# The first two stages of a one-core decoder block, put in order by hand on four engines

## The chip, the cores and the metric

The kernel runs as one program on one core of a Trainium2 chip. The metric is the device time of one execution in microseconds (us), the median of several runs. Engines are named as in the profile: PE (TensorE; PEld is its weight load), DVE (VectorE), ACT (ScalarE), POOL (GpSimd) and SP (SyncE, which here only issues DMAs). DVEq, SPq and so on are the sequencers that issue DMAs.

## What is computed

One transformer block on 256 tokens of width 1024, all in float32. Cut to what matters here:

```
cond = silu(c)                                   # c: 1024
shift_m, scale_m, gate_m, shift_f, scale_f, gate_f = split(cond @ ada_w + ada_b)
h = rmsnorm(x, norm_mix_g) * (1 + scale_m) + shift_m          # 256 x 1024
p = h @ w_in            # q, compressed/selected/window keys and values, gates, MLA parts, merge gates
o_nsa = sparse attention with T5 bias over compressed, selected and window keys
o_mla = latent attention with rotary keys (cos/sin of positions)
x = x + gate_m * ((sigmoid(p.merge_a) * o_nsa + sigmoid(p.merge_b) * o_mla) @ w_o)
h = rmsnorm(x, norm_ffn_g) * (1 + scale_f) + shift_f
x = x + gate_f * (silu(conv3(h @ w_gate)) * (h @ w_up)) @ w_down
return rmsnorm(x, final_norm_g)
```

## The kernel before, in words

Activations lie transposed: 8 tiles of 128 channels by 256 tokens. Every product is made from three matmuls in a reduced float32 form: each operand is split into a high part (a rounding copy, on ACT) and a low part (operand minus high part, on DVE), and `mm3` adds high by high, high by low, low by high.

**Opening.** `par` (a table of biases, norms and c) and the identity (a slice of `cst`) are loaded on ACT's queue, x on SP's in four quarters. From c come `cond` (a tanh on ACT, two operations on DVE), then eight PE matmuls against the identity that spread `cond` over all partitions, then `crow`, their copy out of PSUM. x is squared (ACT), added up (DVE), reduced on PE; the reciprocal root is taken on ACT and POOL (`rstd_col`) and spread over the partitions by a PE matmul (`rstd_bc`, its result `rsp`). Some warm-up matmuls (`busy(WARM[i])`) stand between.

**Stage A, the first projection.** It runs over 8 blocks k of 128 input channels. `modulate(k)` loads two 512 KB pieces of `adaA`, reduces each with `crow` on DVE (`gemv`, an operation of 128x1024), makes the scale `am` and the shift `mod`, then `hf` (x by scale by rsp, DVE), its high part `hh` (ACT) and its low part `hl` (DVE). Then two weight chunks (c = 0, 1) of 128x1024 from `wA` are split into `hi` and `lo`, and each makes 8 tiles of output, 24 matmuls. All 16 output tiles are held in the 8 PSUM banks `accA` (lg, lg, pt, pt, o, mm, mm, ms) until k = 7.

**Evacuation and the values' stage.** The banks are then emptied: `k_evac` (pt banks, keys), `t_evac` (lg banks, inputs of the compressed branch, after which POOL adds position terms), `q_evac` (o, mm, ms banks, queries). The values' stage needs the lg and pt banks again: for 8 blocks k a chunk of 128x560 from `wvg` is split, and 12 matmuls of 280 columns go into four banks (`vps`). The bias table is loaded by four 512 KB DMAs of 1 KB rows from `vdr` (`BT`).

**Mixing stage.** Sparse attention of eight head pairs (`Pair`), with other work (compression with `cw1`, latent projections, merge gates, further `gemv`s) filled in between, then latent attention, the output projection and the gated MLP.

A list scheduler decides the order on every engine before, from priorities (`prio`), dependences and a few `issue_after`s; each engine then runs its list strictly in that order. A tile pool has a fixed number of buffers for a name (`RB = 5` for `raw`, `HB = 3` for `hi` and `lo`); who allocates the next one waits until the oldest is free.

## Time and profile before

| | |
|---|---|
| median of 3 runs | 460.11 us (457.87, 460.11, 460.21) |
| the profiled execution | 458.63 us, of which the span from the first to the last instruction is 456.8 us |
| granted TensorE clock, mean | 0.992 of full speed |
| PE busy | 439.2 us, 96% of the span |
| DVE busy | 366.5 us, 80% |
| ACT busy | 282.3 us, 62% |
| HBM read | 96.01 MB |

Busy time of PE is no measure of its speed, because the matmuls overlap: how many start in a stretch says more. A wait is read from the start times of rows that follow each other on one engine.

### The profile page before, as it was taken

The page shows a single profiled execution, that of the slowest core. Times are in us where ns is not written, and L with a number is a line of the kernel's source. Part 1 is how long each engine was busy: PE and PEld are TensorE (multiplying, and loading weights), DVE is VectorE, ACT ScalarE, POOL GpSimd, SP SyncE. Part 2 cuts the span into 40 slices and gives each one's busy share as a digit, 9 for nine tenths or more (in the row PEclk, how much of TensorE's full clock was granted, in tenths as well). Part 3 has the DMA queues.
Part 4 walks back from the last instruction along what each step waited for, and adds up shares of the span by engine and source line. Part 5 has one row for each costly group of instructions (what it writes and reads, how often), then busy time and mean ns, then how long its engine had stood idle before and what let it go on. Part 6 is the DMA issues. An engine that isn't in the chain of part 4 may idle for free.

```text
span 456.8 us, 9366 instructions
## 1 busy us (share of the span) xinstructions
PE 439.2 (96%) x3514; PEld 414.5 (91%) x3514; DVE 366.5 (80%) x873; ACT 282.3 (62%) x610; POOL 26.2 (6%) x45
## 2 busy tenths in 40 slices
PE   6999989999989999999999999999999999999994
PEld 6899978777869879999989999999999999999993
DVE  3899988878788878899989888778778778778643
ACT  4444475879698996656657776556556556546332
POOL 1100042030010111000000000000000000000001
PEclk9899999999999999999999999999999999999998
DMA  7999898779762337997857875655655655653002
GB/s 279 414 406 377 252 311 238 290 269 297 261 213 95 101 121 250 305 317 254 296 206 220 252 259 189 194 179 178 193 185 168 199 187 165 204 187 93 1 0 93
DMA packets 31565, 99.33 MB, mean 217 GB/s; under 512 B 4293, under 2 KB 6933, under 8 KB 31520
## 3 DMA queue, kind: packets, MB, share of 16 engines
q1 hardware_dynamic: 30208, 96.59, 62.7%
q0 software_dynamic: 1024, 1.98, 1.9%
q8 instruction: 28, 0.46, 0.4%
q10 hardware_dynamic: 288, 0.17, 0.2%
q14 instruction: 17, 0.14, 0.1%
HBM read 96.01 MB, written 1.14 MB: 213 GB/s over the span
## 4 chain that ended last, share of the span: by engine, by line
PE 79%; DVE 6%; DMA 6%; ACT 4%; issue 2%; POOL 1%; DVEq 0%; POOLq 0%; SPq 0%; ACTq 0%
PE mm L176 29%; PE lg L176 12%; PE o L176 12%; PE ms L176 11%; PE pt L176 10%; DMA ad<-in_adaR 3%; DMA cst<-in_cst 2%; PE pt L860 2%; DVE lo L136 2%; DVE ad L377 1%; ACT hi L135 1%; ACT pt L864 1%; PE ms L221 1%; ACT s L608 0%; DVE s L449 0%
## 5 line engine op out<-in xcount | busy, mean ns | idle before, releaser
L176 PE MATMUL mm<-s,hi 128*128 128x256 f32 x552 | 105.2, 288 | 0.6 <-DVE s L991 0.3
L136 DVE TENSOR_TENSOR s<-raw,s 128x1024 fp32r<-128x1024 f32 x66 | 80.5, 1221 | 17.9 <-PE mm L176 14.5
L176 PE MATMUL mm<-s,s 128*128 128x258 f32 (+1 forms) x544 | 94.1, 283 | 0.0
L176 PEld LDWEIGHTS mm<-s,hi 128*128 128x128 f32 x552 | 85.3, 189 | 3.7 <-issue 1.2
L135 ACT ACTIVATE s<-raw 128x1024 fp32r<-128x1024 f32 x66 | 69.0, 1051 | 23.2 <-PE mm L176 23.2
L176 PEld LDWEIGHTS mm<-s,s 128*128 128x128 f32 x544 | 77.6, 189 | 0.1
L176 PE MATMUL mm<-s,lo 128*128 128x256 f32 x268 | 76.9, 287 | 0.1
L136 DVE TENSOR_TENSOR lo<-raw,hi 128x1024 fp32r<-128x1024 f32 (+2 forms) x55 | 63.5, 1161 | 5.6 <-ACT hi L135 5.4
L135 ACT ACTIVATE hi<-raw 128x1024 fp32r<-128x1024 f32 (+2 forms) x55 | 53.5, 989 | 21.0 <-PE mm L176 6.8
L176 PEld LDWEIGHTS mm<-s,lo 128*128 128x128 f32 x268 | 50.5, 188 | 1.5 <-issue 0.7
L176 PE MATMUL o<-s,s 128*128 128x258 f32 (+1 forms) x272 | 47.8, 283 | 0.0
L377 DVE CUSTOM_DVE_ANT_0 ad<-ad,crow 128x1024 f32<-128x1024 f32 x36 | 43.6, 1218 | 3.2 <-DMA ad<-in_adaR 2.9
L176 PE MATMUL ms<-s,s 128*128 128x258 f32 x264 | 46.1, 283 | 0.0
L176 PEld LDWEIGHTS o<-s,s 128*128 128x128 f32 x272 | 39.0, 189 | 0.0
L176 PEld LDWEIGHTS ms<-s,s 128*128 128x128 f32 x264 | 37.7, 189 | 0.0
L176 PE MATMUL lg<-zh,s 128*128 128x256 f32 x176 | 34.7, 280 | 0.0
L176 PE MATMUL pt<-zh,s 128*128 128x256 f32 x176 | 34.6, 279 | 0.0
L839 ACT ACTIVATE L<-L,sm 128x128 f32<-128x128 f32 (+1 forms) x64 | 28.3, 449 | 1.4 <-DVE sm L835 1.4
L176 PEld LDWEIGHTS lg<-zh,s 128*128 128x128 f32 x176 | 28.6, 188 | 0.0
L176 PEld LDWEIGHTS pt<-zh,s 128*128 128x128 f32 x176 | 28.5, 188 | 0.0
L835 DVE CUSTOM_DVE_ANT_0 L<-lg,s 128x128 f32<-128x128 f32 (+1 forms) x64 | 20.9, 350 | 8.6 <-PE lg L176 8.0
L176 PE MATMUL lg<-s,s 128*128 128x256 f32 (+4 forms) x104 | 27.3, 350 | 0.5 <-DVE sm L835 0.5
(250 smaller groups left out, 810.4 us busy)
## 6 DMA issues: line engine op xcount, KB each, us to landing
ad<-in_adaR SPq DMA_DIRECT2D x32, 512.0 KB, 4.6
raw<-in_wg SPq DMA_DIRECT2D x22, 512.0 KB, 3.5
raw<-in_wu SPq DMA_DIRECT2D x22, 512.0 KB, 4.4
raw<-in_wd SPq DMA_DIRECT2D x22, 512.0 KB, 4.5
raw<-in_wA SPq DMA_DIRECT2D x16, 512.0 KB, 8.0
raw<-in_wm SPq DMA_DIRECT2D x16, 512.0 KB, 4.9
L<-in_adaA SPq DMA_DIRECT2D x12, 512.0 KB, 7.9
raw<-in_cw SPq DMA_DIRECT2D x8, 512.0 KB, 5.3
```

Of the source, the lines that this page charges most:

```text
L135: nc.scalar.activation(hi[:], raw[:], AF.Copy)
L136: nc.vector.tensor_tensor(lo[:], raw[:], hi[:], ALU.subtract)
L176: nc.tensor.matmul(o, l, r, start=start, stop=stop, **kw)
L221: m = nc.tensor.matmul(self.ps[:, tt:tt + 1], sq[:, tt * 128:tt * 128 + 128], ones[:, 0:1], start=first and tt == 0, stop=last, skip_group ...
L377: nc.vector.tensor_tensor_reduce(out=ad, in0=ad, in1=crow[:], scale=1.0, scalar=0.0, op0=ALU.mult, op1=ALU.add, accum_out=dst)
L835: nc.vector.tensor_tensor_reduce(out=L[:, br, j, 0:nk], in0=lgj[:, br, :], in1=bias_view(2 * t + j, qt), scale=1.0, scalar=3e38, op0=ALU.a ...
L839: nc.scalar.activation(L[:, br, j, 0:nk], L[:, br, j, 0:nk], AF.Exp, scale=-1.0, bias=sm[:, i:i + 1], accum_out=sm[:, 4 + i:5 + i])
L860: nc.tensor.transpose(pt[:, (kb * 2 + j) * 128:(kb * 2 + j) * 128 + 128], self.L[qt][:, br, j, kb * 128:kb * 128 + 128], ident)
L864: nc.scalar.activation(self.PT[qt, br][:, 0:qt + 1, :], pt[:, 0:(qt + 1) * 256].rearrange("p (b q) -> p b q", b=qt + 1), AF.Copy)
```

## The change

`opening()` and everything from `modulate(0)` to the end of the values' stage stand inside `tc.manual_schedule` for DVE, ACT, PE and SP: on these four engines the instructions run in the order in which the code is written; POOL and all later stages are still ordered by the list scheduler. Inside, the following differ:

- The identity becomes 128 more columns of `par`; one load, first on SP's queue. x comes in two loads.
- `crow` is copied by DVE instead of ACT; four additions of squares instead of five, each reduced on its own; `vec` is made by ACT instead of DVE; the scaled identity of `rstd_bc` by ACT instead of DVE; `am` and `mod` by ACT instead of DVE; `sb1` by POOL with the factor `norm_mix_g` folded in.
- The first six weight chunks are loaded early into other buffers; `HB` is 4.
- For k = 0 all high-by-high matmuls come first, then high-by-low, then low-by-high. The chunks c = 0 of k = 6 and 7 come before their chunks c = 1, so that lg and pt banks are complete 48 matmuls before the others.
- In the values' stage one `q_evac` half and one split stand in each block; the pt banks come first.
- The bias loads `BT` are issued after the third chunk of the values' weights; the tables, later `adaR` loads and `w2k` wait for that stage's end.

```diff
-N_A = 16
-WARM = (6, 3, 4)
+WARM = (5, 2, 2, 3, 3)
-HB = 3
+HB = 4
-EV = "k1 q1 t0 q3 q2 k0 d q0 t1"
-TE = "avvvaaav"
+TE = "aaaavvaa"
...
+        def fetch(early=False):
+            src, cols, _, _ = chunks.pop(0)
+            raw = s4(F32, (128, cols)) if early else st.tile([128, cols], F32, tag="raw", name=nm("raw"), bufs=RB)
+            raws.append([raw])
+            return nc.sync.dma_start(raw[:], src).ins
+        def head():
+            raw = raws[0][0]
+            raws[0] += [st.tile(raw.shape, F32R, tag=t, name=nm(t), bufs=HB) for t in ("hi", "lo")]
+            nc.scalar.activation(raws[0][1][:], raw[:], AF.Copy)
+        def rest():
+            raw, hi, lo = raws.pop(0)
+            nc.vector.tensor_tensor(lo[:], raw[:], hi[:], ALU.subtract)
+            return hi, lo
...
-        nc.scalar.dma_start(par[:], a["par"])
-        nc.scalar.dma_start(ident, a["cst"][:, C_ID:C_ID + 128])
-        for i in range(4):
-            nc.sync.dma_start(xT.t[i // 2][:, i % 2 * 2:i % 2 * 2 + 2, :], a["xT"][:, 2 * i:2 * i + 2, :])
+        ident = par[:, N_PAR:N_PAR + 128]
+        nc.sync.dma_start(par[:], a["par"])
+        for i in range(2):
+            nc.sync.dma_start(xT.t[i][:], a["xT"][:, 4 * i:4 * i + 4, :])
...
+            for c in range(2):
                 ps = bank("pt")
...
-                nc.scalar.activation(crow[:, c * 512:c * 512 + 512], ps[:], AF.Copy)
+                nc.vector.tensor_copy(crow[:, c * 512:c * 512 + 512], ps[:])
+            for h in range(2):
+                busy(WARM[1 + h])
                 for j in range(2):
+                    t = xsq.t[h][:, 2 * j:2 * j + 2, :]
+                    nc.scalar.activation(t, xT.t[h][:, 2 * j:2 * j + 2, :], AF.Square)
+                    nc.vector.tensor_tensor(t[:, 0, :], t[:, 0, :], t[:, 1, :], ALU.add)
+                    ssq.reduce(t[:, 0, :], h == 0 and j == 0, h == 1 and j == 1)
...
-            nc.vector.scalar_tensor_tensor(am[:], mod[:, 8 + k:9 + k], sb1[:, k:k + 1],
-                                           par[:, C_GMIX + k:C_GMIX + k + 1], ALU.add, ALU.mult)
-            nc.vector.tensor_tensor(mod[:, k:k + 1], mod[:, k:k + 1], par[:, C_ADAB + k:C_ADAB + k + 1], ALU.add)
+            nc.scalar.activation(am[:], mod[:, 8 + k:9 + k], AF.Identity, scale=par[:, C_GMIX + k:C_GMIX + k + 1],
+                                 bias=sb1[:, k:k + 1])
...
+            nc.scalar.activation(mod[:, k:k + 1], mod[:, k:k + 1], AF.Identity, bias=par[:, C_ADAB + k:C_ADAB + k + 1])
...
+            for k in range(8):
+                part_hi(k)
...
+                if k < 5:
+                    fetch_ada(k + 3)
+                    fetch()
+                    fetch()
...
+                w = rest()
+                if k:
+                    part_lo(k)
+                head()
+                products(k, 0, w)
+                if k < 6:
+                    w = rest()
+                    head()
+                    products(k, 1, w)
+                if k < 7:
+                    modulate(k + 1, rst[:])
+            fetch()
+            fetch()
+            fetch()
...
+            w = rest()
+            head()
+            products(6, 1, w)
+            w = rest()
+            products(7, 1, w)
...
+            queries = [(i, j) for i in (1, 3, 2, 0) for j in range(2)]
+            for k in range(8):
+                wh, wl = pending.pop(0)
+                if k < 5:
+                    mark = fetch()
+                for tt in (1, 0):
...
+                if k < 6:
+                    head()
+                    pending.append(rest())
+                i, j = queries.pop(0)
+                q_evac(i, (j,))
```

DVE in the opening, before, right behind the two operations on `cond` (`s_6` and `s_7` hold the squares, `L_167` and `L_170` are the two pieces of `adaA` of block 0, each with a read of its sum):

```order
L311 TENSOR_TENSOR s_6_103<-s_6_103 128x256 x3
L311 TENSOR_TENSOR s_6_103<-s_6_103,s_7_104 128x256 x2
L377 ISA L_167,mod<-L_167,crow 128x1024
L377 ISA mod 128x1
L405 TENSOR_SCALAR pt_142<-o_140 16x384
L393 SCALAR_TENSOR_TENSOR am_173<-mod,sb_165,par 128x1
L268 TENSOR_SCALAR sq_149<-cst,rv_146 128x128 x2
L377 ISA L_170,mod<-L_170,crow 128x1024
L377 ISA mod 128x1
L397 SCALAR_TENSOR_TENSOR hf_176<-s_1_74,am_173,ms_152 128x256
L395 TENSOR_TENSOR mod<-mod,par 128x1
L136 TENSOR_TENSOR lo_186<-raw_183,hi_185 128x1024
```

The same place of the changed kernel (`L_113` and `L_115` are those pieces, `s_13` is `hl`):

```order
L310 COPY crow<-pt_165 128x512
L310 COPY crow<-pt_171 128x512
L316 TENSOR_TENSOR s_6_98<-s_6_98 128x256 x2
L316 TENSOR_TENSOR s_7_99<-s_7_99 128x256 x2
L375 ISA L_113,mod<-L_113,crow 128x1024
L375 ISA mod 128x1
L375 ISA L_115,mod<-L_115,crow 128x1024
L375 ISA mod 128x1
L409 SCALAR_TENSOR_TENSOR hf_214<-s_1_74,am_200,ms_208 128x256
L416 SCALAR_TENSOR_TENSOR s_13_108<-hf_214,mod,s_11_106 128x256
L154 TENSOR_TENSOR lo_217<-s_17_117,hi_216 128x1024
L154 TENSOR_TENSOR lo_234<-s_18_119,hi_233 128x1024
```

The additions of squares now stand behind both copies of `crow`, the first `gemv` behind the additions, and `hl` directly behind `hf`; before, it is the row after the last one shown, behind a `lo`.

ACT where stage A ends, before (`hi_686` is the last weight chunk of stage A, `hi_716` and later belong to the values' stage; pt, lg, mm, o, ms are the banks):

```order
L135 ACTIVATE hi_686<-raw_684 128x1024
L135 ACTIVATE hi_716<-raw_714 128x560
L135 ACTIVATE hi_746<-raw_744 128x560
L478 ACTIVATE s_122_786<-pt_198 64x2x256
L478 ACTIVATE s_122_786<-pt_197 64x2x256
L478 ACTIVATE s_123_787<-pt_198 64x2x256
L448 ACTIVATE s_119_783<-mm_200 64x2x256
L462 ACTIVATE s_126_790<-lg_195 64x2x128
L478 ACTIVATE s_123_787<-pt_197 64x2x256
L448 ACTIVATE s_121_785<-ms_202 64x2x256
```

And in the changed kernel, where the chunk of `hi_734` is stage A's last:

```order
L150 ACTIVATE hi_734<-raw_521 128x1024
L469 ACTIVATE s_39_149<-pt_140 64x2x256
L469 ACTIVATE s_39_149<-pt_139 64x2x256
L469 ACTIVATE s_40_150<-pt_140 64x2x256
L469 ACTIVATE s_40_150<-pt_139 64x2x256
L150 ACTIVATE hi_794<-raw_719 128x560
L150 ACTIVATE hi_798<-raw_721 128x560
L455 ACTIVATE s_43_153<-lg_137 64x2x128 x4
L455 ACTIVATE s_44_154<-lg_138 64x2x128 x2
L150 ACTIVATE hi_836<-raw_723 128x560
L441 ACTIVATE s_36_146<-mm_142 64x2x256
L150 ACTIVATE hi_856<-raw_822 128x560
```

All copies out of pt and lg banks now stand ahead of any copy out of o, mm and ms banks, and the latter alternate with the splits of the values' weights.

PE where the values' stage ends, before (the last three rows of `vps`, then the logits of the first head pair and the compression with `raw_948`, a chunk of `cw1`):

```order
L176 MATMUL pt_839<-hi_932,s_17_162 128x280
L176 MATMUL pt_839<-hi_932,s_19_164 128x280
L176 MATMUL pt_839<-lo_933,s_17_162 128x280
L176 MATMUL lg_1039<-s_122_786,s_118_782 128x256
L176 MATMUL lg_1039<-s_124_788,s_118_782 128x256
L176 MATMUL lg_1060<-s_122_786,s_118_782 128x512
L176 MATMUL lg_1060<-s_124_788,s_118_782 128x512
L176 MATMUL ms_1111<-raw_948,s_126_790 64x256
```

And in the changed kernel (`raw_1109` is that chunk of `cw1`):

```order
L193 MATMUL lg_819<-hi_934,s_12_107 128x280
L193 MATMUL lg_819<-hi_934,s_14_109 128x280
L193 MATMUL lg_819<-lo_935,s_12_107 128x280
L193 MATMUL ms_1108<-raw_1109,s_43_153 64x256
L193 MATMUL lg_1036<-s_39_149,s_35_145 128x256
L193 MATMUL lg_1036<-s_41_151,s_35_145 128x256
L193 MATMUL lg_1057<-s_39_149,s_35_145 128x512
L193 MATMUL lg_1057<-s_41_151,s_35_145 128x512
```

The lg banks, which the first logits need, are now the last to be filled, and one matmul of the compression stands ahead of the logits.

## Rows read from the trace of the kernel before

**Rows 1.** The page, part 1: busy us, share of the span, instructions

```profile
PE 439.2 (96%) x3514; PEld 414.5 (91%) x3514; DVE 366.5 (80%) x873; ACT 282.3 (62%) x610; POOL 26.2 (6%) x45
```

**Rows 2.** Windows, stage A and the way to the mixing stage; columns in its first row

```profile
core 0: us, PE busy (x) PEld busy (x) DVE busy (x) ACT busy (x) POOL busy (x), PEclk, DMA share, GB/s
16.20:62.74 46.54, 46.26 (x387) 45.72 (x385) 44.68 (x78) 21.02 (x29) 0.64 (x2) 1.00 0.97 359
62.74:78.67 15.93, 13.50 (x97) 12.68 (x97) 13.96 (x21) 11.08 (x24) 7.50 (x8) 1.00 0.91 225
```

**Rows 3.** Timeline of DVE, opening: start us, us, engine, line, operation

```profile
7.34 0.88 DVE L311 TENSOR_TENSOR s<-s,s 128x256 f32<-128x256 f32 x2
...
10.22 1.23 DVE L377 CUSTOM_DVE_ANT_0 L<-L,crow 128x1024 f32<-128x1024 f32 x1 [1.99 <-ACT crow L300]
...
15.04 0.48 DVE L397 SCALAR_TENSOR_TENSOR hf<-s,am,ms 128x256 f32<-128x256 f32 x1 [0.23 <-PE ms L272]
...
18.52 1.22 DVE L377 CUSTOM_DVE_ANT_0 L<-L,crow 128x1024 f32<-128x1024 f32 x1
```

**Rows 4.** Timeline of all engines, opening: PE and ACT

```profile
6.00 3.55 PE L176 MATMUL pt<-cst,cond 128*128 128x128 f32 x16 [2.01 <-DMA cst<-in_cst]
...
9.59 0.60 ACT L300 ACTIVATE crow<-pt 128x512 f32<-128x512 f32 x1 [0.91 <-PE pt L176]
...
11.85 0.26 ACT L258 ACTIVATE rv<-ms,eps 128x2 f32<-128x2 f32 x1 [1.14 <-PE ms L221]
...
13.83 1.17 PE L272 MATMUL ms<-sq,ones 128*128 128x256 f32 x2
...
15.62 0.51 ACT L398 ACTIVATE s<-hf,mod 128x256 fp32r<-128x256 f32 x1 [2.04 <-DVE mod L395]
```

**Rows 5.** DMA issues of the first 20 us: count, KB, median us to landing

```profile
par<-in_par ACTq DMA_DIRECT2D x1, 101.5 KB, 4.2
```

**Rows 6.** Timeline of DVE, block 7 of stage A

```profile
52.69 1.22 DVE L377 CUSTOM_DVE_ANT_0 L<-L,crow 128x1024 f32<-128x1024 f32 x1
...
54.98 0.21 DVE L393 SCALAR_TENSOR_TENSOR am<-mod,sb,par 128x1 f32<-128x1 f32 x1
...
55.23 0.49 DVE L397 SCALAR_TENSOR_TENSOR hf<-s,am,rst 128x256 f32<-128x256 f32 x1
...
56.77 0.48 DVE L402 SCALAR_TENSOR_TENSOR s<-hf,mod,s 128x256 fp32r<-128x256 f32 x1
```

**Rows 7.** Timeline of PE, end of stage A and values' stage

```profile
57.49 0.28 PE L176 MATMUL lg<-s,hi 128*128 128x256 f32 x1
...
62.46 0.28 PE L176 MATMUL ms<-s,lo 128*128 128x256 f32 x1
...
76.34 0.42 PE L176 MATMUL pt<-hi,s 128*128 128x280 f32 x2
...
77.89 0.42 PE L176 MATMUL pt<-hi,s 128*128 128x280 f32 x2
```

**Rows 8.** Timeline of all engines, values' stage: DVE and POOL

```profile
70.03 3.21 DVE L136 TENSOR_TENSOR lo<-raw,hi 128x560 fp32r<-128x560 f32 x3
...
70.16 1.83 POOL L471 TENSOR_TENSOR s<-s,par 128x512 f32<-128x512 f32 x1
...
74.76 0.68 DVE L449 SCALAR_TENSOR_TENSOR s<-o,s 64x512 fp32r<-64x512 f32 x1
...
76.25 0.69 DVE L449 SCALAR_TENSOR_TENSOR s<-o,s 64x512 fp32r<-64x512 f32 x1
```

**Rows 9.** Timeline of DVE, the first logits of the mixing stage

```profile
80.43 0.29 DVE L835 CUSTOM_DVE_ANT_0 L<-lg,s 128x128 f32<-128x128 f32 x1
```

**Rows 10.** Tile raw, window 56 to 58 us: a chunk queued behind the bias loads

```profile
L116 SPq DMA_DIRECT2D raw<-in_wvg x1: 346/346/346, 56.9 to 56.9; - x1
...
DMA to landing us min/median/max: 6.5/6.5/6.5
```

**Rows 11.** Windows around the fall of TensorE's clock, columns as in rows 2

```profile
10.50:12.69 2.19, 1.93 (x11) 1.28 (x12) 1.05 (x3) 0.63 (x3) 0.50 (x1) 0.99 1.02 419
12.69:16.10 3.41, 3.41 (x15) 3.19 (x15) 3.18 (x9) 1.37 (x3) 0.77 (x2) 0.51 1.03 418
```

More of the change, by code (lines that the diff above doesn't have):

```diff
@@ L220, in reduce @@
                 for tt in range(2):
-                    m = nc.tensor.matmul(self.ps[:, tt:tt + 1], sq[:, tt * 128:tt * 128 + 128], ones[:, 0:1],
-                                         start=first and tt == 0, stop=last, skip_group_check=True)
-                return m.ins
+                    mm(self.ps[:, tt:tt + 1], sq[:, tt * 128:tt * 128 + 128], ones[:, 0:1],
+                       first and tt == 0, last, skip_group_check=True)
             def add(self, t):
@@ new lines, in fetch_ada, with modulate @@
+                nc.sync.dma_start(ads[k, j][:], a["adaA"][k, :, j])
+        hfs = {}
+        def modulate(k, r=None):
+            for j in (1, 0):
+                gemv(mod[:, 8 * j + k:8 * j + k + 1], ads.pop((k, j))[:])
+            am = tp.tile([128, 1], F32, tag="am", name=nm("am"))
+            if r is None:
+                v = rstd_col(ssq, D)
+            nc.scalar.activation(am[:], mod[:, 8 + k:9 + k], AF.Identity, scale=par[:, C_GMIX + k:C_GMIX + k + 1],
+                                 bias=sb1[:, k:k + 1])
+            if r is None:
+                r = rstd_bc(ssq, D, v=v)
+                busy(WARM[4])
+            nc.scalar.activation(mod[:, k:k + 1], mod[:, k:k + 1], AF.Identity, bias=par[:, C_ADAB + k:C_ADAB + k + 1])
+            hfs[k] = t1("hf")
+            nc.vector.scalar_tensor_tensor(hfs[k][:], xT[:, k, :], am[:], r, ALU.mult, ALU.mult)
+            return r
@@ new lines, in part_hi, with part_lo @@
+        def part_hi(k):
+            nc.scalar.activation(hh[:, k, :], hfs[k][:], AF.Identity, bias=mod[:, k:k + 1])
+        def part_lo(k):
+            nc.vector.scalar_tensor_tensor(hl[:, k, :], hfs.pop(k)[:], mod[:, k:k + 1], hh[:, k, :], ALU.add, ALU.subtract)
+        fetch_ada(0)
+        fetch(True)
+        fetch(True)
+        fetch_ada(1)
+        fetch(True)
+        fetch(True)
+        fetch_ada(2)
+        fetch(True)
+        fetch(True)
+        accA = [bank(t) for t in ("lg", "lg", "pt", "pt", "o", "mm", "mm", "ms")]
@@ L439, in body, with q_evac @@
         QS = [s4(F32R) for _ in range(4)]
         KH, KL = [s4(F32R, (128, 2, 2, 256)) for _ in range(2)], [s4(F32R, (128, 2, 2, 256)) for _ in range(2)]
-        def q_evac(i):
-            for j in range(2):
+        def q_evac(i, js):
+            for j in js:
                 ps = accA[4 + i][j * 64:j * 64 + 64, :].rearrange("p (t q) -> p t q", t=2)
@@ L489, in proj, with bias_view, bias_view_c @@
+        def bias_view(h, qt):
+            b = BT[h // 8][h % 8 // 4][:, h % 4, :]
+            return free(b, [[-1, 256]], 255) if qt else free(b, [[-1, 128]], 127)
+        def bias_view_c(g, qt, n):
+            return free(BT[g // 2][g % 2][:, 0, :], [[256, 4], [-16, n]], 224 if qt else 96)
+        for gp in range(2):
+            for K in (KH, KL):
+                nc.gpsimd.dma_start(K[gp][64 - gp * 64:128 - gp * 64], K[gp][gp * 64:gp * 64 + 64])
         def proj():
@@ L539, in ada_rest @@
             o, t, ad = loaded.pop(0)
-            gemv(mod[:, o + t:o + t + 1], ad[:])
+            with tc.issue_after(gv):
+                gemv(mod[:, o + t:o + t + 1], ad[:])
             if len(loaded) < ADB - 1:
@@ L646, in mla_v @@
                         nc.scalar.activation(Vm[tt][:, sl], ps[:], AF.Copy)
-        for i in range(2):
-            nc.sync.dma_start(w2k[:, :, i, :], a["w2k"])
-        nc.sync.dma_start(w2v[:], a["w2v"])
+        with tc.issue_after(mark):
+            for i in range(2):
+                nc.sync.dma_start(w2k[:, :, i, :], a["w2k"])
+            nc.sync.dma_start(w2v[:], a["w2v"])
         KB = cp.tile([128, 4, 2, 16], F32R, name="KB")
```

210 lines of the change are left out of this document (86 added, 124 removed).

## The prediction

> **What bounds the kernel now.** I read the page first: PE is busy 96% of the span [rows 1], so a gain must come from places where PE is fed late, not from less work elsewhere. The windows show where the change works. Stage A and the way from it to the mixing stage take 46.54 and 15.93 us [rows 2]. In the first, 387 matmuls start, one every 0.12 us; in the second only 97, one every 0.164 us.
>
> What is one matmul's own pace? From 57.49 to 62.46 PE starts 43 matmuls of 256 columns without a wait: 4.97/42 = 0.118 us each, so a block of stage A (48) costs PE 5.68 us [rows 7]. A block of the values' stage (12 matmuls of 280 columns), undisturbed, takes 77.89 - 76.34 = 1.55 us; eight take 12.4 [rows 7]. So stage A is already near PE's pace, while the values' stage could begin at 62.58 (62.46 and one step) and be over at 75.0, but the mixing stage begins at 78.67. **3.7 us of waits** lie there, and that is the largest sum in reach.
>
> Then the timelines of DVE and ACT. In stage A, DVE begins a block's first `gemv` at 18.52 and that of block 7 at 52.69: 34.17/6 = 5.70 us per block [rows 3, 6]. DVE at 5.70 and PE at 5.68 are level. In the opening, DVE's chain of `gemv`, `hf`, `hl` and two `lo` decides when block 1 gets its low part; PE's first matmul of block 0, at 16.20, where the first window begins, is early for that.
>
> **The change, part by part.** The sum is made against the profiled execution, 458.63 us (span 456.8 and 1.8 around it). The median shown is 460.11; the profiled one lies between the lowest and the middle run.
>
> *Opening.* `par` landed 4.2 us after its issue at 0.74, at 4.94 [rows 5]; the identity later, since PE waited for it until 6.00 [rows 4]. With both in the first load of SP's queue I take 4.7 (bounds: 0.5 earlier or later, as for the loads around it). The tanh and two operations take the 0.7 us that they take now, less one operation: PE begins at about 5.45 instead of 6.00. Eight matmuls take 3.55, so PE is done at 9.0; the second copy of `crow` (0.60 on ACT [rows 4]; I take 0.65 on DVE, bounds 0.5 and 0.8) ends at 9.65 instead of 10.19. But now the four additions stand behind it, at 0.44 each (0.88 for two [rows 3]): 11.4. The first `gemv` begins there, not at 10.22 [rows 3]; the last reduction (two matmul pairs, about 0.5) lets ACT take the root at 12.0 instead of 11.85 [rows 4]. Behind it stand POOL's power and the scaled identity, as before on one engine or the other, and the spreading matmul, 1.17 from 13.83 [rows 4]; `hf` begins at 15.0 to 15.1, as before (15.04 [rows 3]). From `hf` on DVE has more in its way: `hf` 0.48, wait for `hh` (ACT 0.51 [rows 4]) and two hand-overs of 0.06, `hl` 0.48, two `lo` at 1.14 start to start: 3.9, against 18.52 - 15.04 = 3.48 now. Block 1's first `gemv` begins at 18.9, **0.4 later**. Bounds: 0.9 earlier (identity and `crow` early, the spreading matmul at full clock) to 0.8 later.
>
> *Stage A.* `am` and `mod` leave DVE: 55.23 - 54.98 = 0.25 us per block [rows 6], so DVE needs 5.45. On ACT they cost about 0.26 and 0.2 (the nearest row is the root, 0.26 [rows 4]); ACT is busy 21.02 of 46.54 us [rows 2], and `am` falls under the second `gemv`, so they cost nothing there; without that cover `hf` would wait 0.26 us per block, 2 us in all. DVE then leads, PE paces at 5.68: nothing is won per block. From a block's first `gemv` to the end of `hl` 57.25 - 52.69 = 4.56 passes now [rows 6], 4.31 then. Block 1: low part at 18.9 + 4.3 = 23.2; PE, in strict order, waits there after its first matmul. Blocks 1 to 5 take PE to 51.6. Blocks 6 and 7 then give only their first halves, and DVE needs 4.31 from one to the next: block 7's low part comes at 23.2 + 5 x 5.45 + 4.31 = 54.8, PE is there at 54.45 and waits 0.4. Three halves of 2.84 follow, so stage A's last matmul starts at 63.3 instead of 62.46: **0.8 later** (bounds 0.6 earlier, 1.5 later).
>
> By the Trainium skill, ScalarE: Activation LUTs, section on rules for kernel authors, additions and multiplications belong on VectorE. The trace agrees that each is shorter there. By the rule ACT's extra 0.2 us per block would count, 1.6 in all; by the rows ACT idles over half of the stage.
>
> *Values' stage.* The lg and pt banks are complete 5.68 us before stage A ends, at 57.7. ACT then has 13 operations (four key copies, three splits, six half-bank copies) at 0.51 to 0.60 [rows 4]: 6.9 us, to 64.6. The pt banks and the first split come first and are ready by 61.7, so PE goes on at 63.4 without the break that it has now. After that each block gives DVE a split and a query part, 76.25 - 74.76 = 1.49 us [rows 8], just under PE's 1.55. Against this stands one row: three splits took 3.21 us where 3 x 0.74 are due, 0.98 too long, while POOL's addition beside them took 1.83 [rows 8]. POOL has four such additions, which would now run from about 63.1 on, beside the splits of blocks 2 to 4, in strict order. I stretch three by 0.98: 2.9. The split of block 4 would be done at 68.3 (64.6 + 0.7 + 2 x 1.49) and is due at 69.9 (63.4 + 4 x 1.55 + two matmuls), so 1.6 are spare and PE loses 1.3. Bounds: 0 (the additions fall between the splits) and 2.5. The stage ends at 63.4 + 12.4 + 1.3 = 77.1 instead of 78.67: **1.6 earlier than before in all**.
>
> By the Trainium skill, SBUF — State Buffer, section on the two separate sides, VectorE with two SBUF inputs and a GpSimd operation that reads SBUF exclude each other for a whole instruction. The trace's 0.98 agrees. By the rule alone three splits would each wait up to a whole addition.
>
> *Mixing stage.* Now its first logits reach DVE at 80.43 [rows 9], 1.76 us after PE turned to it, because the tables' work stands ahead on DVE. Afterwards only one conversion does. The last query part ends about 0.4 us after the values' stage, the logits' matmuls and hand-overs take 0.5: logits reach DVE at about 78.0, 2.4 earlier. PE gets a part of the extra 0.8: I take **0.8 earlier** (bounds 0 and 1.7; DVE's work there is the same). The later order differs in places; I take nothing for it, as equal work is moved.
>
> Sum: -1.6 - 0.8 = -2.4 (the 0.8 of stage A is in the first), **456.2 us**, 0.5% under the profiled one.
>
> **Rivals.** *POOL does not disturb* (0.25): splits and additions alternate; the one stretched row is all that speaks against it. Then the values' stage takes 12.4 and the result is 454.9; with an early opening 453.5.
>
> *Given back in the mixing stage* (0.18): PE's first matmul there now needs a chunk of `cw1`, ahead of the logits. Its buffer comes free when the fourth split is done, about 67; a chunk queued behind others landed 6.5 us after its issue [rows 10], at 73.5. If the bias loads and key copies hold it until 79, PE begins as late as now: 458.6 or a little less.
>
> *Slower* (0.10): the bias loads. In SP's queue 2 MB of 1 KB rows stand ahead of the values' chunks 3 and on. A chunk so queued, issued at 56.9, needed 6.5 us [rows 10]; issued at about the same time now, it lands at 63.4, or some 2 us later if the bias loads begin later. PE needs it at 68.0 (63.4 + 3 x 1.55), and 1.4 earlier, at 66.6, to have it split. Every us past that is a us for PE, since ACT and DVE hold everything behind that split. Past 66.6 by 2.4 us the gain is gone; past by 4.7 (71.3) it is slower by 0.5%: I put 461.
>
> *The clock* (0.09): it was granted 0.51, the 1.2 GHz level, from 12.69 to 16.10, after a stretch in which PE started 11 matmul parts in 2.19 us [rows 11]; afterwards PE was busy throughout and it rose. Now PE has little between 12.0 and 13.8. Each us at 1.2 GHz costs stage A half a us; 1.5 are spare ahead of block 1 (PE would be done with block 0 at 21.7, the low part comes at 23.2). Low until 20 would cost 0.4, low until 23 1.9: 458.1. The Trainium skill, TensorE: Matmul & The Clock Gate, Part 1, says that activity releases the low level; the rise in this trace agrees.
>
> **How the numbers follow.** The forecast itself has 0.38 (455 to 457.5). 0.5% of this kernel, 2.3 us, is about what a measurement can tell from no change, so 456.2 lies on that edge; the runs before, their median 1.5 above the profiled one, put a gain of 2.4 a little to the faster side. Faster: all of the first rival, most of the forecast and a third of the clock's case, 0.25 + 0.30 + 0.03 = 0.58. Slower: the bias loads and a little of the mixing stage, 0.12. Within 0.5%: 0.30. The range takes the bounds: -0.6 in stage A, -3.7 + 0 in the values' stage and -1.7 in the mixing stage would be 452.6, all late ends together 460; I give 452.8 to 459.8.
>
> **What would show it.** Right: the first `gemv` at 11.2 to 11.6 and block 1's at 18.5 to 19.3; blocks of stage A at 5.68 on PE with DVE idle 0.2 in each; no break on PE between the two stages; the first logits on DVE at 77 to 78.5. Wrong: splits in the values' stage with no stretch (then faster), or PE waiting there for ACT behind a DMA of `wvg`; PE waiting for `cw1` at the mixing stage's start; a second stretch of 0.5 in the clock after 16; a gain at 80 us that is gone by 220, where the order on PE is again that of before.

## The result: 1.4% slower

| | before | changed |
|---|---|---|
| median, runs taken side by side | 460.16 us (457.87 to 463.32) | 466.69 us (464.52 to 467.29) |
| profiled execution, its span | 458.63 us, 456.8 us | 466.78 us, 465.0 us |
| mean granted TensorE clock | 0.992 | 0.976 |

The ratio is 1.0144, 95% interval 1.0103 to 1.0184. I had forecast 456.2 us and a range that ends at 459.8; the time lies above it.

**The page after**, parts 1 and 2 (each digit of part 2 is a fortieth of the span, 11.6 us):

```profile
PE 445.4 (96%) x3516; PEld 418.4 (90%) x3516; DVE 362.9 (78%) x852; ACT 289.1 (62%) x629; POOL 27.0 (6%) x47
PE   7899989999989999999979999999999999999994
PEclk9799998999999999999988999999999999999997
```

PE is as busy as before [rows 1], DVE has less to do. The second line is the one to read: ahead of its last digit, TensorE's clock falls at three places (digits 2, 7, and 21 and 22, some 14, 71 and 242 us), where before it fell at one [rows 11]. Here each of the three follows a stretch in which PE waited (rows below), so each place is one to look at.

**Where the time goes.** One row of ACT per stage, found in both traces, gives the difference (start in us):

| | before | changed | difference |
|---|---|---|---|
| first exponential of the mixing stage | 80.76 | 81.72 | +0.96 |
| first gate tanh of the last heads' loop | 197.95 | 201.67 | +3.72 |
| last copy of the gated sums (`YH`) | 235.08 | 239.64 | +4.56 |
| last `yh` of the output projection | 255.51 | 263.68 | +8.17 |
| end of the span | 456.8 | 465.0 | +8.2 |

So three stretches make it: up to the first logits 1.0 where I had expected -2.4, the mixing and latent stages 2.8, the last heads' loop with the output projection 4.4; the gated MLP costs the same. The border between the last two stretches is not sharp: by PE's rows, with equally many matmuls still to come, the last one ahead of that last copy began 2.8 us late (237.87 against 235.06), so that 1.8 lie ahead of the copy and 5.4 at it and behind it.

**Opening and stage A**, in the windows and the timelines of DVE, POOL and PE (columns as in rows 2 and 3; they answer to rows 2, 3, 4 and 6):

```profile
15.76:63.01 47.25, 47.25 (x386) 47.17 (x386) 45.50 (x67) 28.20 (x48) 2.36 (x7) 0.96 0.92 341
```

```profile
9.64 1.22 DVE L375 CUSTOM_DVE_ANT_0 L<-L,crow 128x1024 f32<-128x1024 f32 x1 [0.47 <-DMA L<-in_adaA]
...
10.79 1.22 DVE L375 CUSTOM_DVE_ANT_0 L<-L,crow 128x1024 f32<-128x1024 f32 x1
...
14.63 0.48 DVE L409 SCALAR_TENSOR_TENSOR hf<-s,am,ms 128x256 f32<-128x256 f32 x1 [2.60 <-PE ms L193]
...
18.47 1.22 DVE L375 CUSTOM_DVE_ANT_0 L<-L,crow 128x1024 f32<-128x1024 f32 x1
```

```profile
10.88 1.70 POOL L272 TENSOR_TENSOR rv<-rv,mhalf 128x2 f32<-128x2 f32 x1 [7.19 <-ACT rv L271]
```

```profile
13.37 1.22 PE L193 MATMUL ms<-sq,ones 128*128 128x256 f32 x2 [2.11 <-ACT sq L279]
```

```profile
45.97 1.22 DVE L375 CUSTOM_DVE_ANT_0 L<-L,crow 128x1024 f32<-128x1024 f32 x1
...
50.19 1.22 DVE L375 CUSTOM_DVE_ANT_0 L<-L,crow 128x1024 f32<-128x1024 f32 x1
...
54.01 0.48 DVE L416 SCALAR_TENSOR_TENSOR s<-hf,mod,s 128x256 fp32r<-128x256 f32 x1
```

The first `gemv` began at 9.64, earlier than the forecast 11.4, because `par` landed 2.3 us after its issue (4.2 before [rows 5]); what it waited for last, 0.47 us, was its piece of `adaA`. POOL's power then took 1.70 us, so `hf` began at 14.63; block 1's first `gemv` began at 18.47, as in [rows 3], block 6's at 45.97, which is (45.97 - 18.47)/5 = 5.50 us per block, and block 7's at 50.19, 2.5 us earlier than before [rows 6]. No wait of PE stands in the window of stage A.

**Values' stage**, timelines of PE, ACT, SP, DVE and POOL (they answer to rows 7 to 9), and the tile `raw` at 57 us (rows 10):

```profile
62.88 0.28 PE L193 MATMUL ms<-s,lo 128*128 128x256 f32 x1
63.01 0.42 PE L193 MATMUL pt<-hi,s 128*128 128x280 f32 x2
...
67.53 0.29 PE L193 MATMUL lg<-lo,s 128*128 128x280 f32 x1
70.22 0.52 PE L193 MATMUL pt<-hi,s 128*128 128x280 f32 x2 [2.40 <-ACT hi L150]
71.00 0.59 PE L193 MATMUL pt<-lo,s 128*128 128x280 f32 x1 [0.26 <-DVE lo L154]
```

```profile
64.66 0.59 ACT L441 ACTIVATE s<-mm 64x512 fp32r<-64x512 f32 x1
69.50 0.67 ACT L150 ACTIVATE hi<-raw 128x560 fp32r<-128x560 f32 x1 [4.25 <-DMA raw<-in_wvg]
```

```profile
54.54 2.08 SPq L521 DMA_DIRECT2D s<-vdr  x4
56.72 1.21 SPq L145 DMA_DIRECT2D raw<-in_wvg  x2
```

```profile
DMA to landing us min/median/max: 12.6/12.6/12.7
```

```profile
81.39 0.29 DVE L905 CUSTOM_DVE_ANT_0 L<-lg,s 128x128 f32<-128x128 f32 x1 [0.20 <-PE lg L193]
```

Stage A ended at 62.9 and PE went on without a break, as forecast. But chunk 3 of the values' weights, issued at 56.72 behind the four bias loads, landed 12.7 us later, at 69.4; ACT could split it only at 69.50. PE stood still from 67.8 to 70.2, and its clock then fell.

**Output projection**, timelines of SP, ACT and PE:

```profile
234.20 0.33 SPq L115 DMA_DIRECT2D raw<-in_wg  x1
```

```profile
238.68 1.06 ACT L134 ACTIVATE s<-raw 128x1024 fp32r<-128x1024 f32 x1 [4.50 <-DMA raw<-in_wg]
239.64 0.40 ACT L1027 ACTIVATE s<-s 128x256 fp32r<-128x256 f32 x1
```

```profile
237.87 0.28 PE L193 MATMUL mm<-s,lo 128*128 128x256 f32 x1
240.09 0.50 PE L193 MATMUL mm<-s,hi 128*128 128x256 f32 x2 [1.94 <-ACT s L1027]
241.38 0.39 PE L193 MATMUL mm<-s,hi 128*128 128x256 f32 x1 [0.79 <-DVE s L1028]
```

The last copy of the gated sums (L1027), which PE needs, stands on ACT behind a split of the first FFN chunk. That chunk was issued at 234.20 and landed at 238.6. The sum itself was ready at 238.3. Before, the copy stood ahead of every such split, and PE's row there was

```profile
235.55 0.84 PE L176 MATMUL mm<-s,hi 128*128 128x256 f32 x3 [0.21 <-ACT s L957]
```

The windows around the falls of the clock (rows 11):

```profile
11.25:13.00 1.75, 0.00 (x1) 0.00 (x0) 0.77 (x2) 0.49 (x3) 1.33 (x1) 1.00 1.01 412
13.00:19.80 6.80, 6.43 (x27) 6.07 (x28) 4.54 (x7) 4.55 (x10) 0.56 (x1) 0.50 1.03 412
70.20:74.30 4.10, 3.82 (x16) 3.60 (x17) 3.94 (x6) 3.49 (x6) 0.00 (x0) 0.60 0.87 193
242.00:248.70 6.70, 6.13 (x29) 5.83 (x29) 5.19 (x11) 4.64 (x8) 0.00 (x0) 0.51 0.61 170
```

From 242 to 248.7 PE starts a matmul every 0.23 us (6.70 / 29), the 1.2 GHz level, where 0.118 is its pace [rows 7]. At that pace the 29 would take 3.4 us; with the wait of 0.57 that lies in the window, the clock cost 2.7. The waits of 1.94, 0.79 and 0.57 are 3.3 together, where before two of 0.2 and 0.3 stood: 2.75 more. The two make the 5.4 above.

### The profile page after: what moved, and what is told of

Read it like the earlier page. It is cut to its first block, busy times and chain, and to the rows that moved or that the text cites. A ratio compares the mean times of both kernels' runs of the same rounds, so it can differ in the third digit from the quotient of the medians.

```text
span 465.0 us, 9372 instructions
## 1 busy us (share of the span) xinstructions
PE 445.4 (96%) x3516; PEld 418.4 (90%) x3516; DVE 362.9 (78%) x852; ACT 289.1 (62%) x629; POOL 27.0 (6%) x47
## 3 DMA queue, kind: packets, MB, share of 16 engines
HBM read 96.01 MB, written 1.14 MB: 209 GB/s over the span
## 4 chain that ended last, share of the span: by engine, by line
PE 73%; DMA 13%; DVE 6%; ACT 4%; issue 3%; POOL 1%; SPq 0%; POOLq 0%; DVEq 0%; ACTq 0%
PE mm L193 30%; PE lg L193 11%; PE ms L193 11%; PE o L193 11%; PE pt L193 8%; DMA s<-in_wA 4%; DMA raw<-in_wvg 3%; PE pt L930 2%; DMA raw<-in_wA 2%; DMA raw<-in_wo 1%; DVE lo L154 1%; DMA ad<-in_adaR 1%; ACT hi L150 1%; DVE L L375 1%; DMA raw<-in_wg 1%
## 5 line engine op out<-in xcount | busy, mean ns | idle before, releaser
L193 PE MATMUL mm<-s,hi 128*128 128x256 f32 x552 | 107.7, 293 | 4.1 <-ACT s L1027 1.9
L193 PEld LDWEIGHTS mm<-s,hi 128*128 128x128 f32 x552 | 87.0, 193 | 8.6 <-ACT s L1027 2.1
L193 PEld LDWEIGHTS mm<-s,lo 128*128 128x128 f32 x268 | 51.6, 194 | 1.3 <-issue 0.8
L134 ACT ACTIVATE hi<-raw 128x1024 fp32r<-128x1024 f32 (+1 forms) x31 | 32.3, 1045 | 19.9 <-issue 16.0
L135 DVE TENSOR_TENSOR lo<-raw,hi 128x1024 fp32r<-128x1024 f32 (+1 forms) x31 | 37.3, 1202 | 1.9 <-ACT hi L134 1.9
```

The lines of the kernel that those rows point to most:

```text
L134: nc.scalar.activation(hi[:], raw[:], AF.Copy)
L135: nc.vector.tensor_tensor(lo[:], raw[:], hi[:], ALU.subtract)
L193: nc.tensor.matmul(o, l, r, start=start, stop=stop, **kw)
```

## The experiments

My theory from this trace: two places in queues cost, the bias loads ahead of chunk 3 on SP, and the FFN's split ahead of the copy on ACT. Rivals: the DMA engines are full at 60 to 75 us in any order; a stall removed is given back later; the fourth buffer (`HB`) does it.

**The split behind the copy** (`split_behind_copy`).

```diff
-                    nc.scalar.activation(hi[:], raw[:], AF.Copy)
+                    with (tc.issue_after(copied[-1]) if late and copied else nullcontext()):
+                        nc.scalar.activation(hi[:], raw[:], AF.Copy)
...
-            nc.scalar.activation(YH[:, h, :], ON[:, h, :], AF.Copy)
+            copied.append(nc.scalar.activation(YH[:, h, :], ON[:, h, :], AF.Copy).ins)
```

> The changed kernel, with one order added on ACT: the first split of the FFN's weights stands behind the last copy of the gated sums instead of ahead of it (ACT waited there 4.50 us for the DMA of in_wg, and PE behind it until 240.09). Theory 1, the place in ACT's queue is what costs: the copy can start at about 238.3, when DVE is done with the sum; PE goes on at 238.8 instead of 240.09 (-1.3), and the half clock that the trace shows from 242 to 249 goes away (6.8 us at half pace, about -2.5 to -3.4). Time 462 to 463.5 if both go, 465.3 if the clock falls all the same. Theory 2, the late weights themselves cost: the other splits of in_wo now wait behind the one for in_wg, PE waits for them instead, and the time stays at 466 to 467.

Measured: 461.6 us, ratio 1.0055 (1.0024 to 1.0086). That is 0.9% off the changed kernel's ratio, about 4 us. The profiled execution, at 464.24, is the slowest of its ten. In it the copy waits for its sum alone, and the clock's low stretch after it is 242.2 to 245.6 instead of 241.7 to 248.5. Theory 1 holds in the main, as the low stretch is shorter and not gone; theory 2 falls, since PE's only named waits from 230 to 250 are 1.1 us for the copy and 0.3 for DVE.

**The bias loads last** (`bias_last`). The loop over `BT` moves from behind the third `fetch()` to behind the last:

```diff
                     mark = fetch()
+                if k == 4:
+                    for i in range(4):
+                        nc.sync.dma_start(BT[i // 2][i % 2][:], bass.AP(tensor=vd.tensor, offset=vd.offset + i * 4 * 384,
...
```

> The changed kernel with the four bias loads issued behind the last of the values' weights instead of ahead of chunk 3. The order of the later stages, which a scheduler makes, changes with it; the first split of the FFN's weights stands behind the copy there too. Theory 1, chunk 3 was late because it stood behind the bias loads: ACT's 4.25 us wait in the values' stage goes, PE runs from 63 to 75.5 or 76.5 without the break at 67.8 to 70.2 and without the half clock after it, and the first logits reach DVE at 77.5 to 78.5 instead of 81.4; with the wo stage repaired as well the time is 458 to 460. Theory 2, the DMA engines were full and any order would be as late: PE waits as long for a chunk, or for the bias at the first logits, and the logits come at 80.5 or later; then only the wo stage gains, 462 to 464.

Measured: 464.54 us, ratio 1.0132 (1.0064 to 1.0201). Windows of the values' stage and of the 10 us behind it, first logits on DVE, and PE's waits from 60 to 92:

```profile
62.41:75.36 12.95, 12.93 (x98) 12.42 (x96) 10.86 (x14) 8.76 (x16) 6.73 (x5) 1.00 0.80 202
75.36:86.00 10.64, 5.81 (x25) 3.33 (x24) 7.85 (x48) 7.59 (x31) 0.00 (x0) 0.90 1.00 335
```

```profile
77.65 0.29 DVE L906 CUSTOM_DVE_ANT_0 L<-lg,s 128x128 f32<-128x128 f32 x1
```

```profile
PE ms L193 <- DMA raw<-in_cw: 2.8, 2, 1.5
```

The profiled execution, at 469.11, is the slowest of its four. Both theories are half right. The break goes and the first logits come at 77.65, within my original 77 to 78.5. But then PE is busy for 5.81 of 10.64 us: of the 4.8 us that it stands still, 2.8 are for `in_cw`, which now stands behind the bias, and the clock falls. What is taken from one load's wait is put on the next.

**Idle matmuls in PE's gap** (`warm_gap`).

```diff
             mm(psv[0:16, 0:384], tabx[:], oneh[:], True, True)
+            busy(6)
```

> The changed kernel with six more idle matmuls of 128 columns ahead of the spreading matmul, in PE's empty stretch from 11.25 to 13.37; nothing else moves. Theory 1, PE's empty stretch brings the clock down and that is hidden: the clock stays at full pace, or falls later, PE is done with block 0 up to 2 us earlier, but the low part of block 7 comes from DVE's chain at 54.0 as now, so stage A ends at 63.0 and the time is 466 to 467. Theory 2, stage A is PE's: it ends at 61.2 to 61.5, and as chunk 3 of the values' weights still lands at 69.5 the gain is lost there again, but it would show in the trace at 61 us. Theory 3: the fall has nothing to do with the empty stretch and the half clock is there from 13 to 20 all the same.

Measured: 467.89 us, ratio 1.0203 (1.0132 to 1.0274). None of the three as written: here the clock fell at 10.7, ahead of the gap, after x had landed late and while the trace has PE executing, so that this fall has no empty stretch just ahead of it; the idle matmuls at the low level then held the spreading matmul up to 15.83, and `hf` to 16.93. The table further down shows what it settled.

**The kernel before with four buffers** (`before_hb4`).

```diff
-HB = 3
+HB = 4
```

> The kernel before with four buffers for the parts of the weights instead of three, as the change also sets; the scheduler's order moves with it, and the first split of the FFN's weights comes one place behind the last copy, ahead of two splits of in_wo. Theory 1, the fourth buffer brings the FFN's split forward: it waits for its DMA on ACT at about 235 to 239, and PE may wait for the splits behind it: 459 to 462. Theory 2, the fourth buffer is harmless and helps the streams: 457 to 459.

Measured: 460.39 us, ratio 1.0018 (0.9993 to 1.0043). In time the fourth buffer alone costs nothing that can be told; the FFN's split stood behind the copy there. But its trace has the mixing and latent stages as long as those of the changed kernel; the rows stand further down.

**The bias loads spread** (`bias_between`), two behind chunk 4 and two behind chunk 6, with the split behind the copy:

```diff
+                if k in (1, 3):
+                    for i in (k - 1, k):
+                        nc.sync.dma_start(BT[i // 2][i % 2][:], bass.AP(tensor=vd.tensor, offset=vd.offset + i * 4 * 384,
...
```

> As the kernel with the split behind the copy (461.6), and the bias loads spread: chunks 3 and 4 of the values' weights, two bias loads, chunks 5 and 6, two bias loads, chunk 7. Theory 1, both loads were wanted and only their order was wrong: PE runs through the values' stage without a break (63 to 75.5), as with the bias loads last, and the bias is there when the first logits want it (77.7 instead of 81.4), so that nothing is late but the first chunk of in_cw; 457.5 to 459.5. Theory 2, PE's start in the mixing stage hangs on in_cw, which is issued behind all that at 75 to 77: PE waits there for it as with the bias loads last (2.8 us, and the clock falls), and the time stays at 461 to 463.

Measured: 464.54 us, ratio 1.0126 (1.0061 to 1.0191). ACT's waits from 60 to 80 and the tile `raw` from 60 to 68:

```profile
ACT hi L151 <- DMA raw<-in_wvg: 4.9, 2, 3.6
```

```profile
DMA to landing us min/median/max: 8.4/8.5/10.0
```

Not one of my two theories: now chunk 7 is late, 10 us after its issue. The rival of full DMA engines gains: the chunks that are queued behind a bias load between 56 and 67 us land 7.8 to 12.7 us after their issue, here and in the changed kernel.

**The same, with two `in_cw` chunks issued early** (`cw_in_front`), right behind the values' weights:

```diff
                     pending.append(rest())
+                if k in (5, 6):
+                    src, cols, _, _ = chunks.pop(0)
+                    pending.append(st.tile([128, cols], F32, tag="raw", name=nm("raw"), bufs=RB))
+                    mark = nc.sync.dma_start(pending[-1][:], src).ins
```

> As bias_between, and the first two chunks of in_cw issued right behind the last of the values' weights, ahead of the small loads. Theory 1: nothing is gained over bias_between, within 1 us, as in_cw was not what PE waited for. Theory 2: PE goes on from the values' stage (about 75.5) without a wait of more than 0.5 us and with no fall of the clock from 80 to 90, 457 to 459, 2 to 4 us under bias_between.

Measured: 465.24 us, ratio 1.0151 (1.0082 to 1.0221), no gain: chunk 7 is late in the same way. Theory 1 holds, and the trace of the run before shows why: from 60 to 92 us PE waited there 2.4 us for the split of chunk 7 and 1.4 for the gates' copy, and for no chunk of `in_cw`.

**The bias loads first** (`bias_first`). Where are the DMA engines idle? From 49 to 58: windows of before, changed and the next kernel but one (DMA share and GB/s are the last two columns):

```profile
49.00:58.00 9.00, 9.00 (x78) 9.00 (x77) 9.00 (x18) 4.43 (x6) 0.00 (x0) 1.00 0.75 228
```

```profile
49.00:58.00 9.00, 9.00 (x78) 8.92 (x77) 7.85 (x11) 4.83 (x8) 0.00 (x0) 1.00 0.48 131
58.00:70.00 12.00, 9.82 (x80) 9.60 (x79) 7.04 (x10) 7.09 (x15) 7.96 (x10) 1.00 1.14 287
```

```profile
49.00:58.00 9.00, 8.80 (x75) 8.59 (x74) 7.87 (x11) 4.84 (x8) 0.00 (x0) 1.00 1.03 348
58.00:70.00 12.00, 12.00 (x96) 11.55 (x94) 9.97 (x14) 9.59 (x19) 8.53 (x10) 1.00 0.70 181
```

The changed kernel leaves them half idle (0.48) while SP stands at `fetch()` waiting for a buffer, and overfills them afterwards (1.14). So:

```diff
-            fetch()
-            fetch()
-            fetch()
             BT = [[s4(F32) for _ in range(2)] for _ in range(2)]
...
             for i in range(4):
                 nc.sync.dma_start(BT[i // 2][i % 2][:], bass.AP(tensor=vd.tensor, offset=vd.offset + i * 4 * 384,
                                                                   ap=[[1, 128], [384, 4], [1, 256]]))
+            fetch()
+            fetch()
+            fetch()
             w = rest()
```

> The changed kernel with the four bias loads issued ahead of the first three chunks of the values' weights instead of behind them; the FFN's first split still stands ahead of the last copy. Theory 1, the DMA engines are full from 60 to 75 (share over 1.0 at 190 to 290 GB/s) and stood idle from 50 to 58 (share 0.60, 162 GB/s), so that whatever stands last in the queue is late, and only loads moved into the idle time help: chunks 3 to 7 land within 5 us, PE runs through the values' stage without a break (63 to 75.5), the first logits reach DVE at 77 to 78 instead of 81.4, and the time is 462 to 464, as the wo stage still loses its 5. Theory 2: the bias loads wait for their buffers and hold the chunks behind them, PE breaks at 63 or 65 for chunks 0 to 2, and the time is 466 or more.

(The share of 0.60 named there is that of 50 to 60 us; from 50 to 58 it is 0.50, at 132 GB/s.)

Measured: 465.29 us, ratio 1.0097 (1.0061 to 1.0132). The values' stage has no break and chunks 3 to 7 land within 3.7 us. The first logits reach DVE at 79.59, 1.8 us earlier than in the changed kernel, though this execution's opening was 1.2 us late. The first exponential follows only at 81.50, since on ACT a split that waits for a chunk of `in_wc` stands ahead of it:

```profile
79.59 0.29 DVE L905 CUSTOM_DVE_ANT_0 L<-lg,s 128x128 f32<-128x128 f32 x1
```

```profile
80.53 1.06 ACT L134 ACTIVATE hi<-raw 128x1024 fp32r<-128x1024 f32 x1 [1.37 <-DMA raw<-in_wc]
81.50 0.39 ACT L909 ACTIVATE L<-L,sm 128x128 f32<-128x128 f32 x1
```

In time the step is small against its uncertainty (1.0144 to 1.0097, the intervals overlap).

**Bias first, and the split behind the copy** (`bias_first_split_behind`).

> As bias_first, with the FFN's first split behind the last copy; on the engines little else moves. Theory 1, the split's place costs as much here as in the changed kernel (5.1): 457 to 459. Theory 2, a stall removed upstream is given back by an order made with modelled times, so that PE waits at another place between 90 and 250: 461 to 464.

Measured, beside the last one on the same chip: 461.13 against 465.29 us, ratio 1.0033 (1.0013 to 1.0054). From 236 to 256 us, first with the split ahead, then behind:

```profile
236.00:256.00 20.00, 16.98 (x128) 16.36 (x127) 16.36 (x28) 13.07 (x21) 0.00 (x0) 0.91 0.52 169
```

```profile
236.00:256.00 20.00, 19.22 (x158) 18.66 (x158) 19.18 (x36) 15.35 (x26) 0.00 (x0) 1.00 0.63 196
```

30 more matmuls start in the same 20 us, 3.5 us of work at 0.118; the second execution's opening was 1.2 us earlier, but from the first gate tanh to the last `yh`, too, it needs 56.35 us instead of 60.29. The split's place is shown a second time, in a kernel where little else moves: the orders of SP and POOL are the same in both.

**And two chunks of `in_cw` early** (`bias_first_cw`), by the edit of the run before `bias_first`, added to the last kernel.

> As bias_first_split_behind, with the first two chunks of in_cw issued right behind the last of the values' weights. If PE's start in the mixing stage hangs on in_cw, PE has no wait over 0.5 us from 75 to 85 and the time is 1 to 3 us under that kernel; if not, it is within 1 us.

Measured: 459.35 us, ratio **0.9976 (0.9956 to 0.9995)**, 1.8 us under the last one. PE's only wait from 75 to 85 above 0.5 us is 0.9, for the gates' copy. But the last kernel, too, had only that wait there (first its row, then this one's):

```profile
77.69 1.09 PE L194 MATMUL lg<-s,s 128*128 128x256 f32 x4 [0.84 <-ACT gate L565]
```

```profile
77.60 1.09 PE L194 MATMUL lg<-s,s 128*128 128x256 f32 x4 [0.91 <-ACT gate L569]
```

So the time came out as forecast and not by the forecast's cause: with the bias first, PE's start did not hang on `in_cw`, and up to 84 us the two run level. What the 1.8 us come from is not shown. This is the one version that is measurably faster than before, by 0.24%, with the upper end of its interval just under 1.

**The power ahead of the second `gemv`** (`pow_between_gemvs`).

```diff
+                if r is None and j:
+                    v0 = rstd_col(ssq, D)
...
+                    nc.vector.tensor_copy(v[:], v0)
```

> As bias_first_cw, with one copy of 2 columns added on DVE between block 0's two gemvs, which waits for POOL's power; nothing else moves. The power took 0.71 us where no gemv ran (before, and in bias_between, where it began at 10.63, 0.02 ahead of the gemv) and 1.0 to 1.7 where it was issued during one; in each of those it ended 0.64 after that gemv did. Theory 1, POOL waits for DVE's whole gemv: with the gemv held back the power takes 0.71, the scaled identity and the spreading matmul follow, and hf begins 1.2 to 1.6 us earlier (at 13.0 to 13.4, with the first gemv at 9.6 to 9.8); in every run so far the values' stage began 48.4 us behind hf, so that it begins at 61.4 to 61.8 instead of 62.9 and the time falls by 1 to 1.5 us, to 457.8 to 458.4. Theory 2, the power is slow of itself or waits for something else: it takes 1 to 1.7 all the same, the second gemv now stands behind it, and hf is 0.5 to 1 us later. Theory 3: hf is earlier and the loads are not, so that the gain ends at a DMA in stage A.

Measured: 458.78 us, ratio 0.9984 (0.9955 to 1.0012). Timelines of POOL and DVE:

```profile
11.08 0.71 POOL L273 TENSOR_TENSOR rv<-rv,mhalf 128x2 f32<-128x2 f32 x1 [7.38 <-ACT rv L272]
```

```profile
11.83 0.17 DVE L403 COPY am<-rv 128x2 f32<-128x2 f32 x1 [0.63 <-POOL rv L273]
11.90 1.22 DVE L376 CUSTOM_DVE_ANT_0 L<-L,crow 128x1024 f32<-128x1024 f32 x1
...
14.03 0.48 DVE L412 SCALAR_TENSOR_TENSOR hf<-s,am,ms 128x256 f32<-128x256 f32 x1 [0.90 <-PE ms L194]
```

The mechanism is theory 1's: 0.71 us. From the power's start to `hf` it is 2.95 us instead of 3.75; x had landed late in this execution, so `hf` is only 0.6 earlier than in the changed kernel and 0.5 than in the last version, and in time there is no difference from the last version that can be told.

**Three pairs of buffers later on**, in the changed kernel (`changed_three_later`) and in the last version (`best_three_later`; one pair is held from the mixing stage to the FFN):

```diff
+        held = [st.tile([128, 1024], F32R, tag=t, name=nm(t), bufs=HB) for t in ("hi", "lo")]
+        for h_ in held:
+            nc.gpsimd.memset(h_[:, 0:1].bitcast(F32), 0.0)
...
+        free_ = tp.tile([128, 1], F32, tag="am", name=nm("am"))
+        for h_ in held:
+            nc.gpsimd.tensor_tensor(free_[:], h_[:, 0:1].bitcast(F32), x1[:, 6, 0:1], ALU.add)
```

> The changed kernel, and one of its four pairs of buffers for the parts of the weights is held from the mixing stage on until the FFN begins (two memsets and two additions of one column on POOL), so that these stages go on with three pairs as before. Its first two stages are the changed kernel's, instruction for instruction; in the wo stage the FFN's first split falls far behind the last copy, as before. Theory 1, what the changed kernel loses behind 82 us (7.2 of its 8.2 us of span) comes from the fourth pair, by way of the order that a scheduler makes: the wo stage regains its 4 to 5, and from the end of the values' stage to the first gate it takes 119.5 to 120.5 us instead of 121.7; 459 to 461. Theory 2, the fourth pair only put the split ahead of the copy, and the mixing stage's loss is chance or something else: 461 to 462.5, as with the split behind the copy. Theory 3: it is not the buffers, 465 to 467.

> As pow_between_gemvs (458.78), with one of the four pairs of buffers held in the same way. Theory 1, the fourth pair costs the mixing and MLA stages 2 to 4 us (123.05 us from the end of the values' stage to the first gate, before 119.41): 120 to 121 there, 456 to 457.5 in all. Theory 2, it does not: 122 to 124 there, and 458 to 460.

Measured: 463.31 us, ratio 1.0104 (1.0053 to 1.0155), and 459.85 us, 1.0025 (0.9992 to 1.0058). With three pairs the split falls behind the copy in the changed kernel too, and the ratio is 0.4% lower, though the intervals overlap. But from the end of the values' stage to the first gate both need 123.4 us (before 119.4, changed 121.7): theory 1 on the mixing stage falls, as holding a pair gives nothing back there.

## Why the prediction was wrong

**Up to the first logits I was 3.4 us off, and the step that failed is the landing of chunk 3.** The slower rival had the mechanism, place and limits (needed at 66.6, breaks even 2.4 us later); its landing, "63.4, or some 2 us later", was wrong. I took 6.5 us from [rows 10], a chunk that was issued 5.4 us behind the first bias load, when by the trace's DMA packets 1.1 of the 2 MB of bias had still to be moved. Here the first bias load was issued 2.2 us ahead, and 1.9 MB had still to be moved: 12.7 us. It landed at 69.4, 2.8 past my limit, which is that rival's "the gain is gone"; the 0.10 that I gave it was far too little. I had priced the SP queue as an order and the DMA engines not at all: that `BT` had moved behind a third chunk stood in both orders; its first load began 3 us later (51.56 to 54.54). The fall of the clock behind the stall (70.2 to 74.3, some 2 us) was not in the rival's price.

**The larger failure is a sentence: "The later order differs in places; I take nothing for it, as equal work is moved."** Equal work, but on strictly ordered engines: 4.4 us in the output projection, of which the two pairs of kernels give back about 4 us by moving one split on ACT behind one copy. The order there had changed and could have been read; I looked at its first two stages only.

The 2.8 us of the mixing and latent stages fall under the same sentence, but their cause is **not settled**. Windows from the end of the values' stage to the first gate, of before, changed and the kernel before with four buffers:

```profile
78.67:197.95 119.28, 116.33 (x917) 97.55 (x916) 97.93 (x346) 97.39 (x288) 11.73 (x22) 1.00 0.67 226
```

```profile
80.12:201.67 121.55, 118.60 (x917) 96.85 (x916) 99.74 (x350) 98.31 (x290) 11.33 (x22) 1.00 0.66 228
```

```profile
79.00:202.41 123.41, 118.75 (x922) 97.79 (x921) 101.73 (x356) 99.98 (x298) 12.12 (x22) 1.00 0.67 227
```

At full clock PE stands still for 2.95 us in both of the first two; it is busy 2.3 us longer with the same 917 matmuls. Every version of the changed kernel needs 2.3 us or more beyond before's 119.4, and three pairs of buffers do not cure it. But the kernel before with four buffers, whose first two stages are not in order by hand, needs 123.5 as well. So neither the order by hand nor the fourth buffer is shown to be the cause, and each of these figures is from one execution.

The rival "given back in the mixing stage" had the result (2.4 us given back) by luck, not by its mechanism: in the changed kernel PE did not wait for `cw1`. 3.4, 2.8 and 4.4 make the 10.6 between 456.2 and 466.8.

**What held.** Block 1's `gemv` at 18.47 (18.5 to 19.3 said; the first one and `par` came earlier than I put them, POOL's power later), stage A's last matmul at 62.9 (63.3), no break between the stages, first logits at 77.65 in the run with the bias last, whose opening was 0.6 us earlier (78.0). The path was the one forecast: DVE's blocks follow in 5.50 us (5.45), without the idle 0.2 in each that I had put, block 7's low part is done at 54.5 (54.8), and three halves of 2.84 us make 63.0. POOL's additions: three splits took 1.57, 1.06 and 1.06 us where 0.74 are due in the last version, 1.5 too long in all; I put 2.9. With 1.6 spare PE lost about 0.6 (the stage takes 12.95 in the versions without a late chunk, 12.4 undisturbed); I put 1.3. Without the late chunk, then, the forecast of the way to the first logits was right to half a us, in part by luck: the first `gemv` 1.8 us early and POOL's power 1.0 us longer than put largely cancelled. By its own terms (the root 0.15 later) `hf` would have come at 15.2, not at 15.0 to 15.1.

**The clock in the opening** fell as that rival said, to 20, but its price of 0.4 does not show. In the profiled executions of all twelve versions of the changed kernel the values' stage begins 48.37 to 48.42 us behind `hf`, whether the clock was low for 3.5 or for 10 us in all, 0.6 or 5 of it behind `hf` (five of them below): DVE's chain sets the pace, and what PE loses falls into time that it has to spare.

| version | `hf` | clock low | values' stage | difference |
|---|---|---|---|---|
| bias_between | 13.05 | 12.5 to 16 | 61.45 | 48.40 |
| changed | 14.63 | 13 to 20 | 63.01 | 48.38 |
| split_behind_copy | 14.63 | 13.5 to 17 | 63.05 | 48.42 |
| bias_first | 15.83 | 10.5 to 21 | 64.20 | 48.37 |
| warm_gap | 16.93 | 10.5 to 17.5 | 65.33 | 48.40 |

## What to carry to other kernels

A stage put in order by hand moves the scheduler's starting point for all that follows: compare the order of the whole program, engine by engine, and look for work that waits for a DMA and stands ahead of work on the critical path. A load's price here was not its own size but what was queued ahead of it: find where the DMA engines idle, and issue the large load there, ahead of small ones that wait for buffers. After each repair ask what is late next; here it was chunk 3, with the bias last `in_cw`, with the bias spread chunk 7. Only with the bias first, the split behind the copy and `in_cw` early did the kernel come out under the one before, and the last of these moves paid for a reason that is not shown.
